# One-hots of the dense gates laid out by pairs of tokens instead of groups of four

## The chip, the cores and the metric

The kernel runs on one core of one Trainium2 chip. The metric is the device time of one execution in microseconds (us), the median of several runs. The three runs of the kernel before gave 1613.13, 1616.25 and 1616.29 us.

## The reference

The reference chains two transformer blocks over 256 tokens of width 1024: differential attention, MLPs, a second attention, and then a hybrid layer whose last part is a mixture of 16,384 one-row experts (PEER). Only that last part matters here. For each token and each of 8 heads it scores two sets of 128 sub-keys, takes the best 16 of each, and from the 256 sums the best 16; a softmax over these gives the gates. An expert is named by a pair (row key, column key), each 0 to 127. The output is the sum over the chosen experts of gate x gelu(x . u) x v:

```
s1, s2   = the scores of the two sub-key sets          # per token, head: 128 each
v1, i1   = top_k(s1, 16);  v2, i2 = top_k(s2, 16)
g, sel   = top_k(v1[:, None] + v2[None, :], 16)        # 16 of 256
gate     = softmax(g);     expert = i1[sel // 16] * 128 + i2[sel % 16]
y        = sum over 8 x 16 of gate * gelu(x . u[expert]) * v[expert]
```

## The kernel before, in words

The kernel doesn't gather experts. It runs all 16,384 of them densely: `peer()` streams the whole matrix `peer_uT` through TensorE, applies gelu, multiplies with a dense matrix of gates G (128 x 128 gates for each token, almost all zero), and streams the whole `peer_v`. Every weight block (128 rows x 1024 columns, 512 KB) is loaded on SP's queue, and split into a high and a low part for a three-product matmul in reduced-precision f32: ScalarE writes `whi` (L415), VectorE writes `wlo` (L417). `proj_F` (L479) runs the first matrix: for each block 8 products `whi` x high part of x (L490) and then 8 pairs `wlo` x high part, `whi` x low part (L494, L495), all with 128 weight columns and 256 moving columns. After each block's products it calls a hook, then `done_w` (which splits the next block that has room), then the functions that wait in `self.late`. There are 16 groups of 8 blocks.

The hook (L2371) advances the generator `routing()` by an amount set by hand (`rates`, L2368; each `yield` states a cost). So the order of the instructions on each engine is fixed when the program is written out, and isn't changed by how long anything takes. The generator first finds the top 16s on VectorE, then for each half of the tokens makes `rt` (L2326 to L2333): for token t and each of its 128 (head, choice) pairs on the partitions, the row key, the column key, and the gate (scaled by 32768) as a high and a low f16. Its third stage builds G, four tokens at a time, 64 times:

- L2355, VectorE: `oh` = (iota equals key), f16, 1024 elements a partition: 2 one-hots of 128, for 4 tokens. `iota` holds each of 0 to 127 four times over.
- L2358, VectorE: `b` = the one-hot of the column key x the gate's high and low part, f16, 1024 elements.
- L2342, TensorE, in `build()`: for each of the 4 tokens two products of 128 x 128 x 128 that add up in PSUM, with the row key's one-hot as the weights and `b` as the moving operand. The token is the innermost index of both tiles, so the 128 elements of an operand lie 4 f16 apart.
- L2343, ScalarE: PSUM to G with the scale taken back.

`oh` and `b` have two buffers each. `build()` of one group is put into `self.late` when the next but one group's one-hots are issued, so it runs on TensorE behind a block's products.

Of the kernel before, what the change touches and what calls it, by code (L numbers as in the profile page):

```python
# [11 lines left out]
F16 = mybir.dt.float16  # L12
# [3 lines left out]
ALU = mybir.AluOpType  # L16
# [4 lines left out]
P = 128  # L21
S = 256
# [26 lines left out]
def consts():  # L49
    f = np.float32  # L50
    u = np.arange(512)
    rel = u - 127
    n = np.maximum(rel, 0)
    nf = np.maximum(n, 16).astype(f)
    large = 16 + (np.log(nf / f(16)) / f(np.log(8.0)) * f(16)).astype(np.int32)
    bucket = np.where(n < 16, n, np.minimum(large, 31))
    oh = np.zeros((33, 512), f)
    ok = rel >= 0
    oh[bucket[ok], u[ok]] = -1.0
    far = np.where(ok, 0.0, BIG).astype(f)  # L60
    q = np.arange(P)[:, None]
    mask = np.where(np.arange(S)[None, :] > P + q, BIG, 0.0).astype(f)
    cend = np.arange(16) * 16 + 31
    cmask = np.zeros((P, 2, 16), f)
    for th in range(2):
        t = th * P + np.arange(P)
        bad = (cend[None, :] > t[:, None]) | (np.arange(16) == 15)[None, :]
        cmask[:, th] = np.where(bad, BIG, 0.0)
    c01 = (cmask == 0).astype(f)
    repl = np.zeros((16, P), f)  # L70
    bd = np.zeros((P, 4, 2), f)
    for h in range(8):
        for i in range(15):
            repl[i, h * 16 + i] = 1.0
        bd[h * 16:h * 16 + 15, h % 4, h // 4] = 1.0
    fa = f(500000.0) ** (-np.arange(0, 16, 2, dtype=f) / f(16))
    fb = f(500000.0) ** (-np.arange(0, 32, 2, dtype=f) / f(32))
    fr = np.zeros((P, 56), f)
    fr[:, 0:8] = fa
    fr[:, 8:24] = fb  # L80
    fr[:, 24:48] = fr[:, 0:24]
    fr[:, 48:56] = fa
    return {
        "c_ident": np.eye(P, dtype=f),
        "c_oh": oh[:32],
        "c_far": np.tile(far[None, :], (16, 1)),
        "c_mask": mask,
        "c_cmask": cmask,
        "c_c01": c01,
        "c_repl": repl,  # L90
        "c_bd": bd,
        "c_freq": fr,
        "c_iota4": np.tile(np.repeat(np.arange(P), 4).astype(np.float16)[None, :], (P, 1)),
        "c_i16": np.tile(np.arange(16, dtype=np.float16)[None, :], (P, 1)),
    }

# [181 lines left out]
class Net:  # L278
# [1884 lines left out]
    def peer(self):  # L2163
# [3 lines left out]
        with ExitStack() as ctx:  # L2167
# [29 lines left out]
            with ExitStack() as c2:  # L2197
                up = c2.enter_context(tc.tile_pool(name="up", bufs=1))
                self.st = c2.enter_context(tc.tile_pool(name="st2", bufs=1))
                iota = up.tile([P, P, 4], F16, name="iota")  # L2200
                nc.gpsimd.dma_start(out=iota, in_=A["c_iota4"].rearrange("p (n t) -> p n t", t=4))
                io16 = up.tile([P, 16], F16, name="io16")
                nc.gpsimd.dma_start(out=io16, in_=A["c_i16"])
                self.mark("P.q")
# [52 lines left out]
                def routing():  # L2257
# [29 lines left out]
                    for th in range(2):  # L2287
                        ix, cv, ci = found[th]
                        nc.vector.tensor_copy(out=ixf, in_=ix)
                        yield 0.3  # L2290
                        nc.vector.tensor_tensor(out=ge, in0=cv, in1=cv[:, :, 0:1].to_broadcast([P, 8, 16]), op=ALU.subtract)
                        nc.vector.tensor_tensor(out=ge, in0=ge, in1=rq[:, th].unsqueeze(2).to_broadcast([P, 8, 16]), op=ALU.mult)
                        nc.scalar.activation(out=ge, in_=ge, func=AF.Exp)
                        self.table(AF.Gelu_apprx_tanh)
                        yield 0.4
                        for j in range(2):
                            if j == 0:
                                nc.vector.tensor_scalar(out=ru, in0=ci, scalar1=4, scalar2=None, op0=ALU.logical_shift_right)
                            else:
                                nc.vector.tensor_scalar(out=ru, in0=ci, scalar1=15, scalar2=None, op0=ALU.bitwise_and)  # L2300
                            nc.vector.tensor_copy(out=rf, in_=ru)
                            yield 0.3
                            for q in range(2):
                                hl = slice(q * 4, q * 4 + 4)
                                nc.vector.tensor_tensor(
                                    out=eq.rearrange("p h k r -> p (h k) r"),
                                    in0=rf[:, hl].rearrange("p h k -> p (h k)").unsqueeze(2).to_broadcast([P, 64, 16]),
                                    in1=io16.unsqueeze(1).to_broadcast([P, 64, 16]), op=ALU.is_equal)
                                yield 1.1
                                hx = ixf.rearrange("p (h j) r -> p h j r", j=2)[:, hl, j]  # L2310
                                nc.vector.tensor_tensor(out=eq, in0=eq, in1=hx.unsqueeze(2).to_broadcast([P, 4, 16, 16]), op=ALU.mult)
                                yield 0.7
                                nc.vector.tensor_reduce(out=sel[:, j, hl], in_=eq, axis=AX.X, op=ALU.add)
                                yield 1.1
                        gs = up.tile([P, 8], F32, tag="gs", name="gs")
                        nc.vector.tensor_reduce(out=gs, in_=ge, axis=AX.X, op=ALU.add)
                        nc.vector.reciprocal(out=gs, in_=gs)
                        nc.vector.tensor_tensor(out=ge, in0=ge, in1=gs.unsqueeze(2).to_broadcast([P, 8, 16]), op=ALU.mult)
                        yield 0.5
                        yield 1.0  # L2320
                        ps = self.bank()
                        for i, s_ in enumerate((sel[:, 0], sel[:, 1], ge)):
                            nc.tensor.transpose(out=ps[:, i * P:(i + 1) * P], in_=s_.rearrange("p h k -> p (h k)"),
                                                identity=self.ident)

                        rt = up.tile([P, 4, P], F16, tag="rt", name="rt", bufs=2)  # L2326
                        gt = t4[:, 320:448]
                        nc.scalar.copy(out=rt[:, 0:2], in_=ps[:, 0:S].rearrange("p (i t) -> p i t", t=P))
                        nc.scalar.activation(out=gt, in_=ps[:, S:384], func=AF.Copy, scale=32768.0)
                        nc.scalar.copy(out=rt[:, 2], in_=gt)  # L2330
                        yield 0.1
                        yield 1.0
                        nc.vector.tensor_tensor(out=rt[:, 3], in0=gt, in1=rt[:, 2], op=ALU.subtract)  # L2333
                        yield 0.2
                        routes.append(rt)

                    def build(th, t0, oh, b):
                        ps = self.bank()
                        for t in range(4):
                            o = ps[:, t * P:(t + 1) * P]  # L2340
                            for i in range(2):
                                nc.tensor.matmul(out=o, lhsT=oh[:, 0, :, t], rhs=b[:, i, :, t], start=i == 0, stop=i == 1)  # L2342
                        nc.scalar.activation(out=G[th][:, :, t0:t0 + 4], in_=ps.rearrange("p (t n) -> p n t", t=4),  # L2343
                                             func=AF.Copy, scale=1.0 / 32768.0)

# [2 lines left out]
                    for th in range(2):  # L2348
                        rt = routes[th]
                        G[th] = gp.tile([P, P, P], F32, tag=f"g{th}", name=f"G{th}")  # L2350
                        for t0 in range(0, P, 4):
                            bc = lambda i: rt[:, i:i + 2, t0:t0 + 4].unsqueeze(2).to_broadcast([P, 2, P, 4])
                            oh = up.tile([P, 2, P, 4], F16, tag="oh", name="oh", bufs=2)
                            b = up.tile([P, 2, P, 4], F16, tag="b", name="b", bufs=2)
                            nc.vector.tensor_tensor(out=oh, in0=iota.unsqueeze(1).to_broadcast([P, 2, P, 4]), in1=bc(0),  # L2355
                                                    op=ALU.is_equal)
                            yield 0.6
                            nc.vector.tensor_tensor(out=b, in0=oh[:, 1:2].to_broadcast([P, 2, P, 4]), in1=bc(2), op=ALU.mult)  # L2358
                            yield 0.6
                            if last:  # L2360
                                self.late.append(lambda a=last: build(*a))
                            last = (th, t0, oh, b)
# [141 lines left out]
```

## Time and profile before

| what | value |
|---|---|
| three runs, median | 1616.25 us (1613.13 to 1616.29) |
| the profiled execution, its own time | 1613.41 us |
| its span, first to last instruction | 1611.6 us, 1.81 us less than its own time |
| mean granted clock of TensorE | 0.997 |
| TensorE matmul busy | 98% of the span |
| VectorE, ScalarE, GpSimd busy | 70%, 51%, 9% |
| L2342, the gate products | 512 of them, from 1054.8 to 1247.8 us |

A row of a timeline gives the start, the time covered, the engine and line, and how many instructions of one kind it merges (x8). PE is TensorE's matmul, PEld its weight load, which overlaps it. Matmuls overlap one another, so the time between the starts of two of them is what one costs, and their duration is more than that: the spacing in a merged row of n is (time covered - duration of one) / (n - 1).

### The profile page before, as it was taken

What the parts mean: (1) busy time and instruction counts of PE and PEld (TensorE: products, weight loads), DVE (VectorE), ACT (ScalarE), POOL (GpSimd) and SP (SyncE); (2) the same over time, 40 slices, a digit from 0 to 9 for tenths busy, and PEclk for the clock granted to TensorE, in tenths of its full rate; (3) what the DMA queues carried; (4) which work ended last, traced back from release to release, by engine and by line L of the source; (5) the groups of instructions that cost most, each with busy time, mean ns of one, the idle gap of its engine ahead of it and who ended that gap; (6) DMA issues with size and microseconds to landing.
All of it is one profiled execution on the core that took longest, in us unless ns stands there. A gap on an engine that the chain in (4) does not pass through costs nothing.

```text
span 1611.6 us, 26809 instructions
## 1 busy us (share of the span) xinstructions
PE 1578.6 (98%) x10433; PEld 1418.9 (88%) x10433; DVE 1124.0 (70%) x2108; ACT 825.5 (51%) x1302; POOL 147.9 (9%) x114
## 2 busy tenths in 40 slices
PE   8999999999999999999999989999999999999999
PEld 7879998897899887787999989999999888888887
DVE  5678675677776757786547997776676666666666
ACT  5664564357456545556454445544544544444443
POOL 2000000001000003000048850000000000000000
PEclk9999999999999999999999999999999999999999
DMA  8535768573486795860547757755455777777774
GB/s 301 195 112 186 254 217 313 191 248 98 129 282 249 256 328 179 290 223 30 200 143 224 231 184 238 229 174 157 146 182 157 243 242 235 247 248 231 243 245 156
DMA packets 100320, 339.91 MB, mean 211 GB/s; under 512 B 11120, under 2 KB 16576, under 8 KB 100192
## 3 DMA queue, kind: packets, MB, share of 16 engines
q1 hardware_dynamic: 91216, 310.09, 58.5%
q10 hardware_dynamic: 5760, 18.58, 3.0%
q0 software_dynamic: 3216, 9.51, 2.0%
q8 instruction: 82, 1.34, 0.3%
q14 instruction: 46, 0.38, 0.1%
HBM read 303.80 MB, written 34.34 MB: 210 GB/s over the span
## 4 chain that ended last, share of the span: by engine, by line
PE 72%; DVE 15%; ACT 5%; DMA 5%; issue 2%; SPq 0%; ACTq 0%; DVEq 0%
PE ps L475 13%; PE ps L477 13%; PE ps L476 13%; PE ps L494 9%; PE ps L490 9%; PE ps L495 9%; PE ps L2342 4%; DVE wlo L417 3%; ACT whi L415 2%; DMA ahead<-w_in 1%; DVE t L2253 1%; DMA ahead<-w_out 1%; DVE t L2248 1%; DVE t L2251 1%; DVE t L2250 1%
## 5 line engine op out<-in xcount | busy, mean ns | idle before, releaser
L415 ACT CAST whi<-raw 128x1024 fp32r<-128x1024 f32 (+1 forms) x454 | 472.8, 1050 | 514.8 <-PE ps L495 203.7
L417 DVE TENSOR_TENSOR wlo<-raw,whi 128x1024 fp32r<-128x1024 f32 x410 | 498.5, 1223 | 295.3 <-ACT whi L415 294.5
L494 PE MATMUL ps<-x,wlo 128*128 128x256 f32 x1920 | 475.3, 283 | 4.8 <-DVE wlo L417 4.5
L495 PE MATMUL ps<-x,whi 128*128 128x256 f32 x1920 | 474.2, 283 | 0.0
L494 PEld LDWEIGHTS ps<-x,wlo 128*128 128x128 f32 x1920 | 368.1, 192 | 6.2 <-DVE wlo L417 6.2
L495 PEld LDWEIGHTS ps<-x,whi 128*128 128x128 f32 x1920 | 368.0, 192 | 0.0
L490 PE MATMUL ps<-x,whi 128*128 128x256 f32 x1920 | 290.7, 287 | 11.3 <-ACT whi L415 5.8
L475 PE MATMUL ps<-whi,x 128*128 128x512 f32 (+1 forms) x738 | 290.9, 394 | 0.8 <-ACT x L554 0.5
L477 PE MATMUL ps<-whi,x 128*128 128x512 f32 (+1 forms) x738 | 286.6, 388 | 1.5 <-DVE x L1376 1.4
L476 PE MATMUL ps<-wlo,x 128*128 128x512 f32 (+1 forms) x738 | 286.1, 388 | 0.3 <-DVE wlo L420 0.3
L490 PEld LDWEIGHTS ps<-x,whi 128*128 128x128 f32 x1920 | 254.4, 192 | 13.4 <-ACT whi L415 7.8
L475 PEld LDWEIGHTS ps<-whi,x 128*128 128x128 f32 x738 | 139.0, 188 | 33.8 <-issue 5.3
L477 PEld LDWEIGHTS ps<-whi,x 128*128 128x128 f32 x738 | 138.8, 188 | 32.4 <-DVE x L1376 2.6
L476 PEld LDWEIGHTS ps<-wlo,x 128*128 128x128 f32 x738 | 139.1, 188 | 27.9 <-DVE wlo L420 0.6
L417 POOL TENSOR_TENSOR wlo<-raw,whi 128x1024 fp32r<-128x1024 f32 x44 | 106.7, 2426 | 70.0 <-ACT whi L415 69.9
L476 PE MATMUL ps<-wlo,hid 128*128 128x512 f32 x256 | 100.9, 394 | 0.4 <-DVE wlo L417 0.4
L477 PE MATMUL ps<-whi,hid 128*128 128x512 f32 x256 | 100.6, 393 | 0.0
L475 PE MATMUL ps<-whi,hid 128*128 128x512 f32 x256 | 100.6, 393 | 0.0
L2355 DVE TENSOR_TENSOR oh<-iota,rt 128x1024 f16<-128x1024 f16 x64 | 44.2, 690 | 42.1 <-PE ps L2342 42.1
L2342 PE MATMUL ps<-b,oh 128*128 128x128 f16 x512 | 68.2, 296 | 0.0
L476 PEld LDWEIGHTS ps<-wlo,hid 128*128 128x128 f32 x256 | 48.1, 188 | 12.0 <-DVE wlo L417 1.2
L475 PEld LDWEIGHTS ps<-whi,hid 128*128 128x128 f32 x256 | 48.1, 188 | 10.9
(397 smaller groups left out, 1492.3 us busy)
## 6 DMA issues: line engine op xcount, KB each, us to landing
raw<-peer_uT SPq DMA_DIRECT2D x128, 512.0 KB, 3.7
raw<-peer_v SPq DMA_DIRECT2D x128, 512.0 KB, 3.6
raw<-w_up SPq DMA_DIRECT2D x64, 512.0 KB, 5.3
raw<-w_down SPq DMA_DIRECT2D x64, 512.0 KB, 4.9
spill<-ga SPq DMA_DIRECT2D x30, 512.0 KB, 6.0
ga<-spill SPq DMA_DIRECT2D x30, 512.0 KB, 4.5
raw<-w_in_a SPq DMA_DIRECT2D x23, 512.0 KB, 5.8
raw<-w_kv SPq DMA_DIRECT2D x16, 512.0 KB, 5.0
```

The costliest lines, as they stand in the source:

```text
L415: (self.hi_eng or nc.scalar.copy)(out=hi[:, :n], in_=raw[:, :n])
L417: eng.tensor_tensor(out=lo[:, :n], in0=raw[:, :n], in1=hi[:, :n], op=ALU.subtract)
L475: mm(out=out, lhsT=lh, rhs=rh, start=start, stop=False, skip_group_check=skip)
L476: mm(out=out, lhsT=lh, rhs=rl, start=False, stop=False, skip_group_check=skip)
L477: mm(out=out, lhsT=ll, rhs=rh, start=False, stop=stop, skip_group_check=skip)
L490: mm(out=outs[o], lhsT=hi[:, sl], rhs=xs.hi(k), start=k == 0 and o % 2 == 0, stop=False, skip_group_check=True)
L494: mm(out=outs[o], lhsT=lo[:, sl], rhs=xs.hi(k), start=False, stop=False, skip_group_check=True)
L495: mm(out=outs[o], lhsT=hi[:, sl], rhs=xs.lo(k), start=False, stop=k == K - 1, skip_group_check=True)
L2248: nc.vector.max_index(out=idx[:, 0:8], in_max=vals[:, 0:8], in_values=src)
L2250: nc.vector.match_replace(out=wk, in_to_replace=vals[:, 0:8], in_values=src, imm_value=-HUGE)
L2342: nc.tensor.matmul(out=o, lhsT=oh[:, 0, :, t], rhs=b[:, i, :, t], start=i == 0, stop=i == 1)
L2355: nc.vector.tensor_tensor(out=oh, in0=iota.unsqueeze(1).to_broadcast([P, 2, P, 4]), in1=bc(0), op=ALU.is_equal)
```

## The change

The innermost index of `iota`, `oh`, `b` and `rt` becomes a pair of tokens in place of four: the four tokens of a build are two pairs, and the pair is an outer index. The 128 elements of each operand of L2342 then lie 2 f16 (4 bytes) apart where they lay 4 f16 (8 bytes) apart. `iota` is half as big. The first ScalarE copy of `rt` becomes two of half the size, and `b` is written by two instructions of 512 elements where there was one of 1024.

```diff
-        "c_iota4": np.tile(np.repeat(np.arange(P), 4).astype(np.float16)[None, :], (P, 1)),
+        "c_iota2": np.tile(np.repeat(np.arange(P), 2).astype(np.float16)[None, :], (P, 1)),
...
-                iota = up.tile([P, P, 4], F16, name="iota")
-                nc.gpsimd.dma_start(out=iota, in_=A["c_iota4"].rearrange("p (n t) -> p n t", t=4))
+                iota = up.tile([P, P, 2], F16, name="iota")
+                nc.gpsimd.dma_start(out=iota, in_=A["c_iota2"].rearrange("p (n t) -> p n t", t=2))
...
-                        rt = up.tile([P, 4, P], F16, tag="rt", name="rt", bufs=2)
+                        rt = up.tile([P, 2, 64, 2, 2], F16, tag="rt", name="rt", bufs=2)
                         gt = t4[:, 320:448]
-                        nc.scalar.copy(out=rt[:, 0:2], in_=ps[:, 0:S].rearrange("p (i t) -> p i t", t=P))
+                        pairs = lambda x: x.rearrange("p (q t) -> p q t", t=2)
+                        for i in range(2):
+                            nc.scalar.copy(out=rt[:, 0, :, i], in_=pairs(ps[:, i * P:(i + 1) * P]))
                         nc.scalar.activation(out=gt, in_=ps[:, S:384], func=AF.Copy, scale=32768.0)
-                        nc.scalar.copy(out=rt[:, 2], in_=gt)
+                        nc.scalar.copy(out=rt[:, 1, :, 0], in_=pairs(gt))
                         yield 0.1
                         yield 1.0
-                        nc.vector.tensor_tensor(out=rt[:, 3], in0=gt, in1=rt[:, 2], op=ALU.subtract)
+                        nc.vector.tensor_tensor(out=rt[:, 1, :, 1], in0=pairs(gt), in1=rt[:, 1, :, 0], op=ALU.subtract)
...
-                                nc.tensor.matmul(out=o, lhsT=oh[:, 0, :, t], rhs=b[:, i, :, t], start=i == 0, stop=i == 1)
+                                nc.tensor.matmul(out=o, lhsT=oh[:, t // 2, 0, :, t % 2], rhs=b[:, t // 2, i, :, t % 2],
+                                                 start=i == 0, stop=i == 1)
...
-                            bc = lambda i: rt[:, i:i + 2, t0:t0 + 4].unsqueeze(2).to_broadcast([P, 2, P, 4])
-                            oh = up.tile([P, 2, P, 4], F16, tag="oh", name="oh", bufs=2)
-                            b = up.tile([P, 2, P, 4], F16, tag="b", name="b", bufs=2)
-                            nc.vector.tensor_tensor(out=oh, in0=iota.unsqueeze(1).to_broadcast([P, 2, P, 4]), in1=bc(0),
-                                                    op=ALU.is_equal)
+                            pr = slice(t0 // 2, t0 // 2 + 2)
+                            oh = up.tile([P, 2, 2, P, 2], F16, tag="oh", name="oh", bufs=2)
+                            b = up.tile([P, 2, 2, P, 2], F16, tag="b", name="b", bufs=2)
+                            nc.vector.tensor_tensor(
+                                out=oh.rearrange("p q i n t -> p (q i) n t"), in0=iota.unsqueeze(1).to_broadcast([P, 4, P, 2]),
+                                in1=rt[:, 0, pr].rearrange("p q i t -> p (q i) t").unsqueeze(2).to_broadcast([P, 4, P, 2]),
+                                op=ALU.is_equal)
                             yield 0.6
-                            nc.vector.tensor_tensor(out=b, in0=oh[:, 1:2].to_broadcast([P, 2, P, 4]), in1=bc(2), op=ALU.mult)
+                            for q in range(2):
+                                nc.vector.tensor_tensor(
+                                    out=b[:, q], in0=oh[:, q, 1:2].to_broadcast([P, 2, P, 2]),
+                                    in1=rt[:, 1, t0 // 2 + q].unsqueeze(2).to_broadcast([P, 2, P, 2]), op=ALU.mult)
                             yield 0.6
```

## Rows read from the trace of the kernel before

**Rows 1.** The page, part 1: busy time, share of the span, instructions.
```profile
PE 1578.6 (98%) x10433; PEld 1418.9 (88%) x10433; DVE 1124.0 (70%) x2108; ACT 825.5 (51%) x1302; POOL 147.9 (9%) x114
```

**Rows 2.** Stretch of the builds: PE, PEld, DVE, ACT, POOL busy, clock, DMA share, GB/s.
```profile
1051.40:1248.60 197.20, 197.16 (x1652) 194.25 (x1652) 137.51 (x176) 95.09 (x135) 0.00 (x0) 1.00 0.52 163
```

**Rows 3.** Chain of waits from 1040 to 1260 us: shares by line, then pieces.
```profile
by line: PE ps L2342 27.7%; PE ps L494 24.0%; PE ps L495 24.0%; PE ps L490 23.9%; PE ps L475 0.2%; PE ps L2323 0.1%; PE ps L476 0.1%; issue 0.0%
...
1054.99 1.89 PE ps L2342 x16
...
1059.75 0.95 PE ps L2342 x8
...
1246.06 2.05 PE ps L2342 x16
```

**Rows 4.** Groups in that stretch: busy us, mean ns, idle before and its releaser.
```profile
L2342 PE MATMUL ps<-b,oh 128*128 128x128 f16 x512 | 68.2, 296 | 0.0
L417 DVE TENSOR_TENSOR wlo<-raw,whi 128x1024 fp32r<-128x1024 f32 x48 | 58.5, 1220 | 14.5 <-ACT whi L415 14.5
L415 ACT CAST whi<-raw 128x1024 fp32r<-128x1024 f32 x48 | 50.7, 1055 | 83.6 <-PE ps L495 83.6
L2355 DVE TENSOR_TENSOR oh<-iota,rt 128x1024 f16<-128x1024 f16 x64 | 44.2, 690 | 42.1 <-PE ps L2342 42.1
L2358 DVE TENSOR_TENSOR b<-oh,rt 128x1024 f16<-128x1024 f16 x64 | 44.1, 689 | 1.1
```

**Rows 5.** Timeline around one double build, from 1104.2 us (start, us covered).
```profile
1104.27 0.28 PE L494 MATMUL ps<-x,wlo 128*128 128x256 f32 x1
...
1104.39 0.28 PE L495 MATMUL ps<-x,whi 128*128 128x256 f32 x1
...
1104.51 2.06 PE L2342 MATMUL ps<-b,oh 128*128 128x128 f16 x16
...
1106.32 1.20 PE L490 MATMUL ps<-x,whi 128*128 128x256 f32 x8
```

**Rows 6.** Timeline of PE in the later stage, 512 moving columns: first and tenth.
```profile
1399.74 0.39 PE L477 MATMUL ps<-whi,x 128*128 128x512 f32 x1
...
1401.78 0.39 PE L477 MATMUL ps<-whi,x 128*128 128x512 f32 x1
```

**Rows 7.** Timeline of L1845: 15 weight columns and 64 moving columns of plain f32.
```profile
684.00 0.62 PE L1845 MATMUL ps<-w2k,hT 128*15 128x64 f32 x8
...
684.46 0.61 PE L1845 MATMUL ps<-w2v,hT 128*15 128x64 f32 x8
```

**Rows 8.** Timeline of L1952: 128 f32 weight columns and only 32 moving columns.
```profile
713.57 1.97 PE L1952 MATMUL ps<-kcT,qkT 128*128 128x32 f32 x16
```

**Rows 9.** Lines L2342, L1845, L1952: ns min/median/max; L2342's wait for VectorE (us, times).
```profile
L2342 PEld LDWEIGHTS <-oh x512: 112/117/137, 1054.8 to 1247.7; 128*128 128x128 f16 x171
...
  DVE b L2358: 0.2, 1
...
L1845 PEld LDWEIGHTS ps<-w2v,hT x8: 96/96/96, 684.4 to 684.8; 128*15 128x15 f32 x8
...
L1952 PE MATMUL ps<-kcT,qkT x16: 276/276/297, 713.6 to 715.3; 128*128 128x32 f32 x16
```

**Rows 10.** Lines L2305 and L2311, f16 on VectorE: ns min/median/max.
```profile
L2305 DVE TENSOR_TENSOR t<-t,io x8: 1217/1219/1227, 964.3 to 1031.1; 128x1024 f16<-128x1024 f16 x8
...
L2311 DVE TENSOR_TENSOR t<-t,t x8: 683/684/685, 967.8 to 1033.9; 128x1024 f16<-128x1024 f16 x8
```

**Rows 11.** Timeline of VectorE from 1055.5 us: one build's b, the next one's oh.
```profile
1056.71 0.69 DVE L2358 TENSOR_TENSOR b<-oh,rt 128x1024 f16<-128x1024 f16 x1
1057.32 0.69 DVE L2355 TENSOR_TENSOR oh<-iota,rt 128x1024 f16<-128x1024 f16 x1
```

**Rows 12.** Lines L2328 and L2330, ScalarE's copies into rt: ns min/median/max.
```profile
L2328 ACT CAST rt<-ps x2: 372/372/373, 1000.0 to 1046.4; 128x256 f16<-128x256 f32 x2
...
L2330 ACT CAST rt<-t x2: 299/300/301, 1000.6 to 1047.0; 128x128 f16<-128x128 f32 x2
```

## The prediction

> **What bounds the kernel now.** I read the page's busy times first: TensorE is busy for 98% of the span, the other engines for 70% or less [rows 1]. That alone proves nothing, since matmuls overlap, so I went to the stretch in which the builds run, 1051.4 to 1248.6 us. [...] The chain of waits through that stretch is TensorE and nothing else: L2342 holds 27.7% of 220 us, 60.9 us, or 119 ns for each of 512 products [rows 3]. VectorE does wait for TensorE, 42.1 us in front of `oh` [rows 4], and TensorE waited once for `b`, 0.2 us [rows 9]. So what a gate product costs on TensorE is paid in full, and VectorE's time is not, as long as it keeps ahead.
>
> What sets 119 ns? The 16 products of a double build cover 2.06 us, which is (2.06 - 0.296) / 15 = 117.6 ns from start to start [rows 4, 5]. Two things could set it: reading 128 weight columns, or streaming 128 moving columns.
>
> - The weights. A load lasts 112 to 137 ns, median 117 [rows 9], suspiciously like the spacing. But a load's duration is not its price, since loads overlap: L1845's loads last 96 ns each [rows 9], and its products follow one another every (684.46 - 684.00) / 8 = 57 ns [rows 7]. Where the load is the bound, 128 plain f32 weight columns against 32 moving ones, the spacing is (1.97 - 0.276) / 15 = 113 ns [rows 8, 9].
> - The moving columns. The reduced f32 products, whose neighbours lie 4 bytes apart, take 120 ns for 256 columns [rows 5] and (1401.78 - 1399.74) / 9 = 226.7 ns for 512 [rows 6]: (226.7 - 120) / 256 = 0.417 ns a column, and 13 ns that don't depend on the columns. L2342 takes 117.6 ns for 128 columns, (117.6 - 13) / 128 = 0.82 ns a column: twice as much, at twice the distance between neighbours. I take the distance to be the cause.
>
> **The change, part by part.**
>
> *L2342's moving operand at 4 bytes.* No row has f16 at that distance. The nearest are the reduced f32 products, with the same distance: 13 + 128 x 0.417 = 66.7 ns. The lower bound is 57 ns, L1845's spacing with half the columns [rows 7]; the upper bound is 112 ns, the shortest f16 load seen [rows 9], if loads do stand in line. I take 67, since those rows share distance, weight width and neighbourhood. The saving is 117 - 67 = 50 ns for each product that has another gate product behind it. The pieces of the chain show 30 single builds (x8, 0.95 us) and 17 double ones (x16, 1.89 us), 47 bursts [rows 3]; the last product of each is followed by L490, whose f32 weights take 113 ns to read [rows 8] and can begin only when that last product begins. So that one costs at least 113 ns in any case, against some 120 now; 0.5 us at most over 47 bursts, which I leave out of the sum and keep for the range. So 512 - 47 = 465 products x 50 ns = **23.3 us less**. With 57 ns it is 27.9 us, with 112 ns 2.3 us.
>
> [...]
>
> *L2342's weights at 4 bytes.* Their read is hidden now behind the moving columns, by the argument above, and can only get cheaper. Nothing.
>
> *`oh`, 1024 elements, innermost run 2 instead of 4.* Now 690 ns [rows 4]. f16 with a run of 16 or 4 takes 684 to 690; with one operand repeated element by element (a run of 1) it takes 1219 [rows 4, 10]. A run of 2 has no row; both ends are bounds. It still gives two neighbours for each step, like 4, so I take 690.
>
> *`b` in two instructions.* From f32 to f16 the same 1024 elements fall from 1220 to 690 ns [rows 4], which is 512 steps of 1.035 ns saved and leaves 160 ns that don't depend on the count; so 512 elements take 160 + 265 = 425 ns, and two 850. An instruction that doesn't need its predecessor starts 80 ns before that one ends (1056.71 + 0.69 against 1057.32) [rows 11], so a build's VectorE time rises by some 0.16 - 0.08 = 0.08 us, 5 us in all. It lies under TensorE: VectorE's work in the stretch becomes 137.5 + 5 = 143 us of 197 - 23 = 174, 82%. Its slack is smaller, and what would be late next is `b` or `wlo` in front of TensorE. In three blocks there are 4 builds: TensorE needs 3 x 2.88 + 4 x 0.55 = 10.8 us (24 products of 120 ns a block), VectorE 4 x 1.42 + 3 x 1.14 = 9.1. `b` is issued a block ahead of its build, `wlo` three ahead. ScalarE stays at 95 us. I cost both at nothing.
>
> *`rt`.* One copy of 372 ns becomes two of 300 [rows 12], twice in the kernel, on a ScalarE that mostly waits, before the builds begin; 0.46 us, hidden behind proj_F's products. The strided output might make them slower; the cover is some tens of us. The `iota` load on POOL's queue moves half the bytes, long before use. Nothing.
>
> **Sum.** 1613.41 - 23.3 = 1590.1 us against the profiled execution, whose own time is 2.84 us under the median; from the median it is 1593.0. I put the forecast between them, at 1591. A difference of 0.2%, 3.2 us, is about what a measurement of this kernel can tell from no change; the three runs shown span that much.
>
> **Rivals.**
>
> 1. *Something smaller sets the new spacing* (a weight load, or a fixed cost per pair), between 75 and 112 ns. For: the load's 117 ns equals the spacing. Against: L1845 at 57. It gives 465 x 42 to 465 x 5, or 20 to 2 us less: 1593 to 1614.
> 2. *The distance is not what costs.* Every reduced f32 row is also of another type and width; 0.82 ns a column could belong to f16 with any step, and plain f32 in L1845, packed, takes 57 / 64 = 0.89 ns a column as well [rows 7]. Then L2342 stays at 117 ns, the extra VectorE time is hidden, and the time stays at 1613 to 1616. [...] The trace's 0.82 against 0.417 ns a column speaks against it, without proving it.
> 3. *Slower: VectorE falls to one element per step.* If a run of 2 is treated like the run of 1 in L2305, `oh` takes 1219 ns and each half of `b` 690 (160 + 512 x 1.035), 2.6 us a build. VectorE then has 58.5 + 64 x 2.6 = 225 us, less 14 us for some 177 starts that overlap by 80 ns, 211 us in a stretch of 197, and becomes the bound: some 14 us more, 1627 us. It decides from (197 - 58.5) / 64 = 2.16 us a build. Against it: two neighbours are there to be read together.
>
> **How the numbers follow.** The main case (spacing 57 to 75 ns, no stall) gets 0.66: 1585 to 1597. Rival 1 gets 0.14, nearly all of it still faster. Rival 2 gets 0.12, rival 3 0.08. Faster by over 0.2%: 0.66 + 0.14 = 0.80; same 0.12; slower 0.08. The low end is 1613.13 - 27.9 - 0.5 = 1585, the high end takes in rival 1 down to a saving of 9 us (1616 - 9 = 1607), and leaves out rivals 2 and 3, which hold the 2 in 10.
>
> **What would show it.** Right: 16 gate products in a row cover about 0.3 + 15 x 0.067 = 1.3 us where they cover 2.06; L2342 falls from 60.9 to some 38 us of the chain; TensorE still waits for neither `b` nor `wlo`; the two halves of `b` take 425 ns each and `oh` 690; all that comes before 1050 us and after the builds keeps its length. Wrong: the spacing stays near 117 (rival 2) or falls only to the load's duration (rival 1); or `oh` takes 1.2 us and L2342 or L494 wait for VectorE (rival 3).

## The result, and the profile after

The kernel after takes 1585.71 us (median of 4 runs, 1584.5 to 1589.82), where the kernel before took 1614.69 beside it (4 runs, 1612.66 to 1616.29): 29.0 us less, a ratio of 0.9826 with a 95% interval of 0.9802 to 0.9849. The forecast was 1591 us, 1585 to 1607, for a saving of 23.3. So the result lies 5 us under the forecast and only just inside the range; one of the four runs (1584.5) is below its low end.

The profiled execution took 1586.47 us. First the stretch of the builds, with the same columns as [rows 2]: the window from just before the first `oh` to just behind the last gate product is 169.2 us long, where it was 197.2.

```profile
1052.50:1221.70 169.20, 168.92 (x1653) 166.70 (x1652) 141.44 (x240) 92.54 (x135) 0.00 (x0) 1.00 0.61 188
```

TensorE (first number) still fills it, and VectorE's 141.4 us (third number) are now 84% of it. The stretch behind it, some 350 us long, is the same in both kernels; first the kernel before, then the one after:

```profile
1248.60:1600.00 351.40, 351.40 (x1593) 292.58 (x1593) 235.22 (x257) 170.81 (x198) 0.00 (x0) 1.00 0.71 237
1221.70:1573.00 351.30, 351.30 (x1593) 292.38 (x1593) 235.20 (x257) 171.27 (x198) 0.00 (x0) 1.00 0.72 237
```

So the difference arises in the stretch of the builds. What comes before it took 1.1 us longer in the profiled execution of the kernel after (first `oh` at 1052.6 against 1051.5 us), so the two profiled executions differ by 26.9 us only. That start moves from trace to trace, from 1050.0 to 1054.1 us over the runs below, whose instructions up to there are the same but for `iota` and `rt`. The groups of the window of 169.2 us, the counterpart of [rows 4] (lines from 2326 on have moved; L2342 is now L2344, L2355 is L2358, L2358 is L2364):

```profile
L417 DVE TENSOR_TENSOR wlo<-raw,whi 128x1024 fp32r<-128x1024 f32 x48 | 58.6, 1220 | 9.3 <-ACT whi L415 9.3
L2364 DVE TENSOR_TENSOR b<-oh,rt 128x512 f16<-128x512 f16 x128 | 48.5, 421 | 1.1
L2358 DVE TENSOR_TENSOR oh<-iota,rt 128x1024 f16<-128x1024 f16 x64 | 44.1, 690 | 16.5 <-PE ps L2344 16.3
L2344 PE MATMUL ps<-b,oh 128*128 128x128 f16 x512 | 38.1, 221 | 0.3 <-DVE b L2364 0.3
```

The 512 gate products keep TensorE busy for 38.1 us where it was 68.2, and one lasts 221 ns where it lasted 296. `oh` still takes 690 ns with its run of 2, and a half of `b` 421. VectorE's wait for TensorE in front of `oh` has gone from 42.1 to 16.3 us: that is its slack, and TensorE waits once for `b`, 0.3 us. The weight loads of the line (ns min/median/max), the counterpart of [rows 9]:

```profile
L2344 PEld LDWEIGHTS <-oh x512: 96/97/102, 1056.0 to 1220.9; 128*128 128x128 f16 x171
```

And a single build in TensorE's timeline, with the same columns as [rows 5]:

```profile
1102.42 0.64 PE L2344 MATMUL ps<-b,oh 128*128 128x128 f16 x8
1102.87 1.19 PE L490 MATMUL ps<-x,whi 128*128 128x256 f32 x8
```

(0.64 - 0.22) / 7 = 60 ns from start to start; over all 465 pairs of starts in the trace the mean is 59.7 (median 58), where it was 117.0. That makes 465 x 57.3 = 26.6 us. From the start of a burst's last product to the second L490 behind it the trace has 226 ns where it had 251: 47 x 25 ns = 1.2 us more. The two make 27.8 us, and from the first gate product to the last the trace has indeed 165.0 us in place of 193.0. The chain of waits from 1040 to 1232 us, after:

```profile
by line: PE ps L490 28.5%; PE ps L494 27.7%; PE ps L495 27.4%; PE ps L2344 16.0%; PE ps L2323 0.2%; DVE b L2364 0.2%; issue 0.0%; DVEq L417 0.0%
...
1056.13 0.95 PE ps L2344 x16
1057.08 1.00 PE ps L490 x8
1059.99 0.48 PE ps L2344 x8
```

L2344 has 16.0% of 192 us, 30.7, where L2342 had 60.9 [rows 3]; a double build takes 0.95 us in place of 1.89. The 30.2 us between the two are more than the 28.0 that the stretch lost, since L490 took some of it over: it had 23.9% of 220 us, 52.6, and has 28.5% of 192, 54.7.

### The profile page after: what moved, and what is told of

The parts are those of the page before. It is cut to its first block, busy times and chain, and to the rows that moved or that the text cites. A ratio compares the mean times of both kernels' runs of the same rounds, so it can differ in the third digit from the quotient of the medians.

```text
span 1584.7 us, 26875 instructions
## 1 busy us (share of the span) xinstructions
PE 1551.7 (98%) x10433; PEld 1393.8 (88%) x10433; DVE 1127.3 (71%) x2172; ACT 823.5 (52%) x1304; POOL 147.7 (9%) x114
## 4 chain that ended last, share of the span: by engine, by line
PE 71%; DVE 15%; DMA 5%; ACT 5%; issue 2%; SPq 0%; ACTq 0%; DVEq 0%
PE ps L475 13%; PE ps L477 13%; PE ps L476 13%; PE ps L490 9%; PE ps L494 9%; PE ps L495 9%; DVE wlo L417 2%; PE ps L2344 2%; ACT whi L415 2%; DMA ahead<-w_in 1%; DVE t L2253 1%; DMA pre<-ahead 1%; DVE t L2248 1%; DVE t L2251 1%; DVE t L2250 1%
## 5 line engine op out<-in xcount | busy, mean ns | idle before, releaser
L415 ACT CAST whi<-raw 128x1024 fp32r<-128x1024 f32 (+1 forms) x454 | 473.2, 1050 | 498.9 <-PE ps L477 205.2
L490 PE MATMUL ps<-x,whi 128*128 128x256 f32 x1920 | 290.9, 287 | 10.1 <-ACT whi L753 5.9
L490 PEld LDWEIGHTS ps<-x,whi 128*128 128x128 f32 x1920 | 254.0, 192 | 11.8 <-ACT whi L753 5.9
L476 PEld LDWEIGHTS ps<-wlo,hid 128*128 128x128 f32 x256 | 48.1, 188 | 11.6 <-DVE wlo L417 0.7
L475 PEld LDWEIGHTS ps<-whi,hid 128*128 128x128 f32 x256 | 48.1, 188 | 10.9
L477 PEld LDWEIGHTS ps<-whi,hid 128*128 128x128 f32 x256 | 48.1, 188 | 10.8
L2358 DVE TENSOR_TENSOR oh<-iota,rt 128x1024 f16<-128x1024 f16 x64 | 44.1, 690 | 16.5 <-PE ps L2344 16.3
```

The source lines that it names most:

```text
L415: (self.hi_eng or nc.scalar.copy)(out=hi[:, :n], in_=raw[:, :n])
L475: mm(out=out, lhsT=lh, rhs=rh, start=start, stop=False, skip_group_check=skip)
L476: mm(out=out, lhsT=lh, rhs=rl, start=False, stop=False, skip_group_check=skip)
L477: mm(out=out, lhsT=ll, rhs=rh, start=False, stop=stop, skip_group_check=skip)
L490: mm(out=outs[o], lhsT=hi[:, sl], rhs=xs.hi(k), start=k == 0 and o % 2 == 0, stop=False, skip_group_check=True)
L2358: nc.vector.tensor_tensor(out=oh.rearrange("p q i n t -> p (q i) n t"), in0=iota.unsqueeze(1).to_broadcast([P, 4, P, 2]), in1=rt[:, 0, pr] ...
```

## The experiments

Theory M is the prediction's: the distance between neighbours of the moving operand sets a gate product's price. Theory W is that the weight load does. The change moved both operands, so the result alone can't tell them apart.

**The moving operand at 4 bytes, the weights back at 8** (the line numbers of this kernel and the next are 2 higher, L2346)

```diff
+  of, bf = (x.rearrange("p q i n t -> p (q i n t)") for x in (oh, b))
...
-  nc.tensor.matmul(out=o, lhsT=oh[:, t // 2, 0, :, t % 2], rhs=b[:, t // 2, i, :, t % 2],
+  l = of[:, 0:512].rearrange("p (n s) -> p n s", s=4)[:, :, t]
+  nc.tensor.matmul(out=o, lhsT=l, rhs=b[:, t // 2, i, :, t % 2],
                    start=i == 0, stop=i == 1)
```

> The kernel after the change, with the weights of the gate products read 4 f16 (8 bytes) apart again and the moving operand left at 4 bytes. The products read the wrong one-hots, the work is otherwise the same. Theory M (the moving operand's distance sets the spacing): spacing stays near 58 ns, the time stays within 3 us of the kernel after, 1585. Theory W (the weight load's distance sets it): spacing near 117 ns, the time goes back to about 1613.

Measured: 1587.97 us (4 runs, 1587.08 to 1591.47), a ratio to the kernel before of 0.9845 (0.9829 to 0.9862). Its loads and products (ns min/median/max), and a single build in TensorE's timeline:

```profile
L2346 PEld LDWEIGHTS <-oh x512: 111/113/137, 1056.0 to 1222.5; 128*128 128x128 f16 x171
L2346 PE MATMUL ps<-b,oh x512: 217/221/253, 1056.0 to 1222.6; 128*128 128x128 f16 x171
...
1102.89 0.66 PE L2346 MATMUL ps<-b,oh 128*128 128x128 f16 x8
```

The loads last 113 ns, the products stay at 221, and the spacing is (0.66 - 0.22) / 7 = 63 ns where it was 60: over all pairs of starts the mean is 62.5 (median 60). The interval overlaps that of the kernel after, so the run times don't show a difference. The traces do, a small one: from the first gate product to the last it takes 166.6 us in place of 165.0. So some 1.6 of the 29 us hang on the weights, by one execution of each kernel; the run over the weights' distances below shows as much for each product.

**The weights at 4 bytes, the moving operand back at 8**

```diff
+  of, bf = (x.rearrange("p q i n t -> p (q i n t)") for x in (oh, b))
...
-  nc.tensor.matmul(out=o, lhsT=oh[:, t // 2, 0, :, t % 2], rhs=b[:, t // 2, i, :, t % 2],
+  r = bf[:, i * 512:(i + 1) * 512].rearrange("p (n s) -> p n s", s=4)[:, :, t]
+  nc.tensor.matmul(out=o, lhsT=oh[:, t // 2, 0, :, t % 2], rhs=r,
                    start=i == 0, stop=i == 1)
```

> The kernel after the change, with the moving operand of the gate products read 4 f16 (8 bytes) apart again and the weights left at 4 bytes. The products read the wrong gates, the work is otherwise the same. Theory M: spacing 107 to 118 ns, 465 x 50 to 59 = 23 to 27 us more than the kernel after, 1609 to 1613. Theory W: spacing near 58, 1585.

Measured: 1614.51 us (10 runs, 1610.64 to 1619.78), a ratio to the kernel before of 1.0003 (0.9991 to 1.0016). That is 1.5 us above the expected 1609 to 1613, within the spread of its runs.

```profile
L2346 PEld LDWEIGHTS <-oh x512: 96/117/120, 1057.5 to 1249.7; 128*128 128x128 f16 x171
L2346 PE MATMUL ps<-b,oh x512: 274/297/301, 1057.5 to 1249.8; 128*128 128x128 f16 x171
...
1106.96 2.04 PE L2346 MATMUL ps<-b,oh 128*128 128x128 f16 x16
```

(The last line is from TensorE's timeline.) The products last 297 ns again and a double build covers 2.04 us, where it was 2.06 before the change. VectorE's instructions, the copies into `rt` and the weights are those of the kernel after, and nothing of the gain is left. Theory W falls: the moving operand's distance alone decides over the gain, and the weights' 1.6 us show only while that distance is small. The loads last 117 ns here, as before the change, though the weights lie 4 bytes apart. So that duration needs no wide step of the weights.

**How the price goes with the distance**: successive builds read the moving operand 1 to 8 f16 apart, each from a line of its own (L2349 for 1, L2351 for 2, and on to L2363 for 8)

```diff
-  nc.tensor.matmul(out=o, lhsT=oh[:, t // 2, 0, :, t % 2], rhs=b[:, t // 2, i, :, t % 2],
-                   start=i == 0, stop=i == 1)
+  of, bf = (x.rearrange("p q i n t -> p (q i n t)") for x in (oh, b))
...
+  r = lambda s: bf[:, 0:P * s].rearrange("p (n s) -> p n s", s=s)[:, :, 0]
+  mm = nc.tensor.matmul
+  c = t0 // 4 % 8 + 1
+  if c == 1:
+      mm(out=o, lhsT=oh[:, t // 2, 0, :, t % 2], rhs=r(1), start=i == 0, stop=i == 1)
...
+  if c == 8:
+      mm(out=o, lhsT=oh[:, t // 2, 0, :, t % 2], rhs=r(8), start=i == 0, stop=i == 1)
```

> The kernel after the change, with the moving operand of successive builds read 1, 2, 3, 4, 5, 6, 7, 8 f16 apart (2 to 16 bytes), the weights left at 4 bytes; the products read the wrong gates. Measured so far: 58 ns at 4 bytes, 117 at 8. Theory of bytes (the columns cost in proportion to the bytes passed over, from 4 bytes up): 58, 58, about 83, 112 to 117, 140, 165, 190, 215 ns. [...] Theory of two classes (up to 4 bytes fast, anything above half): 58, 58, then 112 to 117 for all the others.

A single run, 1622.47 us. One build of each distance in TensorE's timeline (start, us covered):

```profile
1055.62 0.62 PE L2349 MATMUL ps<-b,oh 128*128 128x128 f16 x8
1056.08 0.63 PE L2351 MATMUL ps<-b,oh 128*128 128x128 f16 x8
...
1059.46 0.88 PE L2353 MATMUL ps<-b,oh 128*128 128x128 f16 x8
...
1061.63 1.09 PE L2355 MATMUL ps<-b,oh 128*128 128x128 f16 x8
...
1066.89 1.32 PE L2357 MATMUL ps<-b,oh 128*128 128x128 f16 x8
...
1068.03 1.56 PE L2359 MATMUL ps<-b,oh 128*128 128x128 f16 x8
...
1072.31 1.77 PE L2361 MATMUL ps<-b,oh 128*128 128x128 f16 x8
...
1076.80 1.99 PE L2363 MATMUL ps<-b,oh 128*128 128x128 f16 x8
```

The duration of a single product of the shortest and of the longest distance, and of the longest's weight load (ns min/median/max):

```profile
L2349 PE MATMUL ps<-b,oh x64: 219/219/232, 1055.6 to 1235.9; 128*128 128x128 f16 x64
...
L2363 PEld LDWEIGHTS <-oh x64: 96/118/120, 1076.8 to 1255.0; 128*128 128x128 f16 x64
L2363 PE MATMUL ps<-b,oh x64: 389/409/411, 1076.8 to 1255.2; 128*128 128x128 f16 x64
```

From all the starts in the trace, the median spacing is 56, 58, 89, 116, 146, 173, 201 and 229 ns for 2, 4, 6, 8, 10, 12, 14 and 16 bytes. 2 and 4 bytes cost the same to 2 ns; from 4 bytes on each further 2 bytes cost 27 to 31 ns for 128 columns, in proportion to the bytes passed over (58 x bytes / 4 gives 87, 116, 145, 174, 203 and 232). The theory of bytes holds, at prices up to 7% above those expected (229 for 215 at 16 bytes); that of two classes falls at 6 bytes (89, not 116) and above 8. The weight load, 4 bytes apart throughout, lasts 118 ns at a spacing of 229: that a load of 117 ns and a spacing of 117 ns stood side by side before the change was chance.

**The same for the weights**: successive builds read them 1, 2, 4, 8 f16 apart, the moving operand at 4 bytes

```diff
-  nc.tensor.matmul(out=o, lhsT=oh[:, t // 2, 0, :, t % 2], rhs=b[:, t // 2, i, :, t % 2],
-                   start=i == 0, stop=i == 1)
+  of, bf = (x.rearrange("p q i n t -> p (q i n t)") for x in (oh, b))
...
+  l = lambda s: of[:, 0:P * s].rearrange("p (n s) -> p n s", s=s)[:, :, 0]
+  mm = nc.tensor.matmul
+  c = t0 // 4 % 4
+  if c == 0:
+      mm(out=o, lhsT=l(1), rhs=b[:, t // 2, i, :, t % 2], start=i == 0, stop=i == 1)
...
+  if c == 3:
+      mm(out=o, lhsT=l(8), rhs=b[:, t // 2, i, :, t % 2], start=i == 0, stop=i == 1)
```

> The kernel after the change, with the weights of successive builds read 1, 2, 4, 8 f16 apart (2 to 16 bytes) and the moving operand left at 4 bytes; the products read the wrong one-hots. If the load is hidden behind the moving columns, the spacing is 58 ns for 1, 2 and 4, and only the load's duration moves (97 ns at 2, about 112 to 117 at 4). If it grows in proportion to the distance, 8 f16 may come out from behind and show a spacing above 58.

A single run, 1588.02 us. L2349, L2351, L2353 and L2355 are distances of 1, 2, 4 and 8 f16 (ns min/median/max):

```profile
L2349 PEld LDWEIGHTS <-oh x128: 95/96/100, 1055.7 to 1217.6; 128*128 128x128 f16 x128
...
L2351 PEld LDWEIGHTS <-oh x128: 96/97/98, 1056.1 to 1218.0; 128*128 128x128 f16 x128
...
L2353 PEld LDWEIGHTS <-oh x128: 111/113/133, 1059.5 to 1222.4; 128*128 128x128 f16 x128
L2353 PE MATMUL ps<-b,oh x128: 217/221/248, 1059.5 to 1222.5; 128*128 128x128 f16 x128
L2355 PEld LDWEIGHTS <-oh x128: 142/144/168, 1061.5 to 1222.0; 128*128 128x128 f16 x128
L2355 PE MATMUL ps<-b,oh x128: 219/225/282, 1061.5 to 1222.0; 128*128 128x128 f16 x128
```

The load's duration grows by 16 ns from 4 to 8 bytes and by 31 more to 16; from all the starts in the trace, the products' median spacing is 58, 58, 60 and 64 ns, with some longer ones at 8 and 16 bytes (mean 59, 58, 63 and 71). So the load stays nearly hidden behind 128 moving columns: at 8 bytes it shows with some 3 to 5 ns a product, at 16 with some 12. The load's duration doesn't hang on its own distance alone: with the moving operand 8 bytes apart it was 117 ns at 4 bytes too.

**What of a product doesn't depend on its columns**: builds cut into pieces of 128, 64 and 32 moving columns (8, 16, 32 products); the pieces all write anew, so the two parts of the gate aren't added

```diff
-  nc.tensor.matmul(out=o, lhsT=oh[:, t // 2, 0, :, t % 2], rhs=b[:, t // 2, i, :, t % 2],
-                   start=i == 0, stop=i == 1)
+  mm = nc.tensor.matmul
+  c = t0 // 4 % 3
+  r = b[:, t // 2, i, :, t % 2]
+  l = oh[:, t // 2, 0, :, t % 2]
+  if c == 0:
+      mm(out=o, lhsT=l, rhs=r, start=True, stop=True)
+  if c == 1:
+      for h in range(0, P, 64):
+          mm(out=o[:, h:h + 64], lhsT=l, rhs=r[:, h:h + 64], start=True, stop=True)
+  if c == 2:
+      for h in range(0, P, 32):
+          mm(out=o[:, h:h + 32], lhsT=l, rhs=r[:, h:h + 32], start=True, stop=True)
```

> The kernel after the change, with the products of successive builds cut into pieces of 128, 64 and 32 moving columns (8, 16, 32 products a build), all writing anew; so the high and low parts are not added. The fixed part of a product: if it is the 13 ns of the reduced f32 products, the slope is (58 - 13) / 128 = 0.35 ns a column, and 64 columns take 35 ns, 32 take 24. If it is near 5 ns, the slope is 0.417 ns and 64 columns take 31, 32 take 18, unless the weight load (97 ns long, overlapping) sets a floor that then shows as the same spacing for 64 and 32.

A single run, 1595.53 us. TensorE's timeline, a build of each width (L2349 for 128 columns, L2352 for 64, L2355 for 32):

```profile
1057.04 0.64 PE L2349 MATMUL ps<-b,oh 128*128 128x128 f16 x8
...
1068.12 0.66 PE L2352 MATMUL ps<-b,oh 128*128 128x64 f16 x16
1068.61 0.95 PE L2355 MATMUL ps<-b,oh 128*128 128x32 f16 x32
```

The durations of the two shorter kinds (ns min/median/max):

```profile
L2355 PE MATMUL ps<-b,oh x640: 176/177/191, 1060.9 to 1225.9; 128*128 128x32 f16 x160
L2352 PE MATMUL ps<-b,oh x352: 190/192/205, 1057.5 to 1229.5; 128*128 128x64 f16 x176
```

64 columns: (0.66 - 0.192) / 15 = 31 ns, median of all starts 30. 32 columns: (0.95 - 0.177) / 31 = 25 ns. Between 128 and 64 columns the slope is (58 - 30) / 64 = 0.44 ns a column, and what remains is some 2 ns; with the 31 ns of the build shown it is 0.42 and some 4. The 13 ns of the expectation fall (64 columns would take 35); its other case, near 5 ns and 31 for 64 columns, lies within what the trace can tell. At 32 columns that case had 18 ns, and 25 were measured: something else sets it, and what that is was not tried. How far loads overlap shows in the kernel after: 97 ns each, and a product with its load every 58 ns.

**VectorE's extra instruction alone**: the kernel before, with `b` written in two halves

```diff
-  nc.vector.tensor_tensor(out=b, in0=oh[:, 1:2].to_broadcast([P, 2, P, 4]), in1=bc(2), op=ALU.mult)
+  for i in range(2):
+      nc.vector.tensor_tensor(out=b[:, i], in0=oh[:, 1], op=ALU.mult,
+                              in1=rt[:, 2 + i, t0:t0 + 4].unsqueeze(1).to_broadcast([P, P, 4]))
```

> The kernel before, with b written by two VectorE instructions of 512 elements (the high and the low part of the gates) in place of one of 1024; nothing else. Theory of the prediction (VectorE's extra 0.08 us a build lies under TensorE): no difference to the kernel before within 0.2%, 1613 to 1616, and no wait of TensorE for b. Rival (VectorE's time shows): 64 x 0.08 = 5 us more.

Measured: 1613.78 us (10 runs, 1611.02 to 1617.38), a ratio of 0.9995 (0.9985 to 1.0006). In the window of [rows 2]:

```profile
1051.40:1248.60 197.20, 197.16 (x1652) 194.31 (x1652) 142.04 (x240) 94.70 (x135) 0.00 (x0) 1.00 0.52 163
```

VectorE is busy for 142.0 us where it was 137.5, the 5 us of the prediction; from the first gate product to the last it takes 193.0 us in both, and TensorE never waits for `b`. The second instruction is paid for out of VectorE's waiting.

**How much cover is left after**: the kernel after, with each half of `b` written twice

```diff
-  for q in range(2):
+  for q in (0, 1, 0, 1):
```

> The kernel after the change, with each half of b written twice: four instructions of 512 elements a build in place of two. VectorE's busy time in the stretch of the builds was 141 us of 169 (measured after); the extra 128 x 0.34 us = 44 make 185. If TensorE bounds only as long as VectorE's sum is smaller than TensorE's, VectorE becomes the bound and the stretch grows to about 185, 16 us more than the kernel after: about 1601. Rival (buffers and order leave enough cover): within 3 us of 1585.

Measured: 1605.68 us (4 runs, 1600.42 to 1607.37), a ratio to the kernel before of 0.9954 (0.9937 to 0.997), which is 20 us more than the kernel after and 5 more than the 1601 expected. The profiled execution is the fastest of the four (1600.42 us). Waits between 1050 and 1250 us (engine, line waited for: us in total, times, longest); the load and its product wait for the same `b`:

```profile
PEld L2344 <- DVE b L2364: 14.4, 15, 2.5
PE ps L2344 <- DVE b L2364: 11.6, 15, 2.3
```

The window from the first to the last gate product, with the columns of [rows 2]:

```profile
1053.30:1235.20 181.90, 170.29 (x1620) 164.98 (x1619) 177.84 (x360) 92.05 (x134) 0.00 (x0) 0.99 0.55 170
```

And the builds' groups on VectorE in that window, with the columns of [rows 4]:

```profile
L2364 DVE TENSOR_TENSOR b<-oh,rt 128x512 f16<-128x512 f16 x251 | 89.5, 418 | 1.1
L2358 DVE TENSOR_TENSOR oh<-iota,rt 128x1024 f16<-128x1024 f16 x62 | 42.3, 682 | 0.0
```

From the first to the last gate product it takes 181.9 us, VectorE is busy for 177.8 of them (98%), and TensorE now waits for `b` 15 times, 11.6 us. `oh` no longer waits for TensorE at all (0.0). VectorE is the bound. The whole stretch, from just before the first `oh` to just behind the last gate product (1049.9 to 1235.6 us), is 185.7 us long, as the sum 185 had it, against 169.2 in the kernel after: 16.5 us more. So the cover of the kernel after is real but thin: 169.2 - 141.4 = 28 us, 0.43 us a build, and the extra work, 181.2 - 141.4 = 40 us of VectorE's time in that stretch, went past it.

## Why the prediction was right, and where its sum was short

- *TensorE's time for a gate product is paid in full.* Right. The 27.8 us that the gate products and the L490 behind them lost are the loss of the whole stretch, 28.0.
- *The distance of the moving operand's neighbours sets 117 ns.* Right, and now shown: taking it back alone takes the whole gain back (1.0003), taking the weights' distance back alone leaves all but 1.6 us of it.
- *The term of 67 ns was mis-sized; it measured 58* (59.7 with the first product of each burst). The step that failed is the 13 ns "that don't depend on the columns", carried over from the reduced f32 products: f16 has some 2 to 4 ns. The slope, 0.417 ns a column, held (0.42 to 0.44). With 117 - 59.7 in place of 117 - 67 the sum is 26.6 in place of 23.3 us. The bound from L1845, 57 ns, came nearer by luck: it is half the columns, of plain f32, at twice the price a column (0.89 ns).
- *The weights at 4 bytes: nothing.* Nearly right: some 1.6 us, by the traces of the run that takes them back.
- *The last product of a burst can fall by 0.5 us in all at best.* It fell by 1.2: less the 120 ns of an L490, a burst's last product cost 251 - 120 = 131 ns before, not 120, and costs 226 - 120 = 106 now, less than the 113 taken from L1952. That the load of L490's weights sets the 106, as the prediction has it, is argued; in both traces that load starts 1 to 2 ns behind the burst's last product, but no run varied it.
- *VectorE.* `oh` 690 as forecast, a half of `b` 421 for 425, busy 141.4 us for 143. TensorE waited for `b` once, 0.3 us, where the forecast had nothing.
- *ScalarE's copies into `rt`.* 268 ns each for 300, four of them; nothing of it shows.
- *Rival 1* (a weight load or a cost per pair sets a spacing between 75 and 112 ns) falls: 58 ns with a load for every product, and 25 ns with 32 columns.
- *Rival 2* (f16 costs 0.82 ns a column at any distance) falls with the run over the distances: 56 ns at 2 bytes, 58 at 4, 229 at 16.
- *Rival 3* (VectorE at one element per step) falls with `oh` at 690 ns. That VectorE can become the bound was shown all the same: with four instructions for `b` it was busy for 98% of the 181.9 us.

So the range held because it reached down to L1845's 57 ns; the sum itself was 5.7 us short, 3.3 of them by the 13 ns and 1.2 by the last products. The rest of the 29.0 us, some 1 us, lies within the spread of the runs (3.6 us before, 5.3 after); the start of the builds alone moves by 4 us from trace to trace. Why the reduced f32 products carry 13 ns that f16 doesn't was not tried.

## What to carry to other kernels

When a matmul takes f16 operands cut out of a larger tile (no other 16-bit type was run), look at the distance between neighbours of the moving operand: up to 4 bytes it costs next to nothing (58 ns against 56 at 2), and from there the product's time grows with the bytes passed over, 14 ns a byte for 128 columns, up to the 16 bytes tried. The weights forgive far more (8 bytes apart cost some 3 to 5 ns a product of 128 moving columns; fewer columns were not tried), so if one operand must be the wide one, let it be the weights. And an interleave of two f16 elements is enough: it keeps VectorE's writes at the rate of four (`oh` at 690 ns) and TensorE's reads at 58 to 60 ns.

## What the runs showed that was not expected

- A weight load's duration says little about what it costs: 97 ns of load with a product every 58 ns in the kernel after, 113 ns with one every 60 where the weights lie 8 bytes apart, and 118 ns with one every 229 where the moving operand lies 16 bytes apart. Nor does it hang on the weights alone: 4 bytes apart, they loaded in 97 ns beside a moving operand at 4 bytes and in 117 beside one at 8.
- f16 products go down to 25 ns apart at 32 moving columns; from 64 columns (30 ns) to 128 (58) the price goes with the columns.
- Six bytes between neighbours cost 89 ns, between the 58 at 4 bytes and the 116 at 8: the price goes by bytes.
